# Adding the experts' rows to x: loads with adds on two engines, replaced by accumulating DMAs

## The chip, the cores and the metric

The kernel runs on one core of a Trainium2 chip. The metric is the device time of one execution in microseconds (us); lower is better. Everything is computed in float32.

## The reference, cut to what matters

Two blocks on 1024 tokens of 1024 numbers. The first block (a state-space layer, pooling, a gated unit and a dense FFN) and the first half of the second one (convolution and gated linear attention) are the same in both kernels. What the change touches is the end: a hierarchical mixture of experts, with a residual and a layer norm.

```
x = layer_norm(...)                         # 1024 tokens x 1024
gl = x @ w_group                            # softmax over 8 groups, one group a token
el = x @ w_expert, in the chosen group      # 8 experts, the best two (k = 0, 1)
for each token and its two experts e, weight w:
    h   = silu(x @ Wg[e]) * (x @ Wu[e])     # 1024 -> 512
    ffn += w * (h @ Wd[e])                  # 512 -> 1024
out = layer_norm(ALPHA * x + ffn) * g + b
```

There are 64 experts, each with 6.3 MB of weights (three matrices of 1024 x 512), so 403 MB in all.

## The kernel before, in words

**Sets.** The experts run in 30 sets, in the order of the string `ORDER` (line 33). A letter is a kind of set: F has the two experts that are fixed, D one expert with room for 256 tokens, S one expert with 128 tokens, P two experts with 64 tokens each, Q four experts with 32 tokens each. Which experts these are is found at run time, from the counts. The last five sets are P Q S S Q.

**Weights.** SP issues all weight loads, in the order of the sets, into a ring of eight chunks of 2 MB (`E.chunk`). A load into a chunk waits until the matmuls that read its former content are through. For a Q set the third matrix comes in 16 pieces of 512 KB by k (the call with `by_k`, line 1967). What stands behind a waiting load on SP waits as well.

**One set.** `fetch` gathers the next set's tokens from DRAM (`take`, an indirect DMA on POOL's queue) into one of two tiles `xg0`, `xg1`; `turn` transposes them on PE to `xT`. `hidden` does the gate and up products (`pg`, `pu`, line 1997), ACT the Silu (line 2004), DVE the product (line 2005). `rows` transposes h (`ph`, line 2013; copies to `hT`, lines 2016 and 2017), does the down-projection (`py`, line 2022) and scales the rows by the tokens' weights.

**Where the rows go.** For the first 27 sets ACT writes the scaled rows to a tile y, and `put` (line 1677) scatters y to the DRAM array `y2d`, in which token t has two rows, 2t for k = 0 and 2t + 1 for k = 1. The last `NLATE` = 3 sets don't scatter: their rows are added to x by products with a one-hot matrix S on PE (`spread`, its adds from PSUM on DVE at line 2052). For the last set of all only its own tokens' sums are wanted, in PSUM (`px`).

**Adding y2d to x.** Ahead of the weights of the penultimate set, `add(c)` runs for c = 0 to 3: SP loads 2 x 1 MB of y2d into a chunk of the ring (line 2102), and DVE and POOL add the two rows of each token to the eight tiles of x in SBUF (`xr`, 128 tokens each; line 2106).

**Norms and the end.** In the last set, `norms(range(4))` stands ahead of `hidden` and `norms(range(4, 8))` behind it. For each tile: two statistics and an aggregate on DVE (line 2119), a scaled copy by ACT into `xg0` or `xg1` (line 2126), a product by a row of gains (`io`) on DVE (line 2127), a sum with a row of offsets (`xT`) on POOL (line 2128), a store on POOL's queue (line 2129). So two tiles are in flight at a time. Last come the last set's tokens: their sums in `px` are normalised (line 2202) and scattered over the rows that the stores wrote (line 2206). Two loops behind this (`further` and the one at line 2213) serve experts with more tokens than their room; with the data here neither runs.

**Order on an engine.** A scheduler orders each engine's instructions by what it estimates of their times. It is not the order in which the code is written: instructions of `norms` can stand behind those of `hidden`.

Of the kernel before, what the change touches and what calls it, by code (L numbers as in the profile page):

```python
# [11 lines left out]
F32 = mybir.dt.float32  # L12
F32R = mybir.dt.float32r
BF = mybir.dt.bfloat16
I32 = mybir.dt.int32
# [3 lines left out]
P = 128  # L19
# [10 lines left out]
NLATE = 3  # L30
KINDS = {"F": (62, 64, 2), "D": (0, 2, 1), "S": (2, 12, 1), "P": (12, 30, 2), "Q": (30, 62, 4)}
CUT = (4,)
ORDER = "FQDPPQDPPQSSPQSQSPSQSPSPSPQSSQ"
# [1647 lines left out]
def route(tc, K, RT):  # L1681
# [225 lines left out]
    K.io, K.io128 = K.A4("io"), io128  # L1907
# [36 lines left out]
def experts(tc, I, K, out):  # L1944
# [64 lines left out]
    def rows(R, h, parts, w, between=lambda t, bank: None):  # L2009

        ph = PT("ph")
        for k in range(4):
            pe.transpose(ph[:, k * P:(k + 1) * P], h[:, k * P:(k + 1) * P], ident)
        hT = Z("hT", (P, 4, P), bufs=2)
        p4 = ph.rearrange("p (k t) -> p k t", k=4)
        dve.tensor_copy(hT[:, 0:2], p4[:, 0:2])
        dve.tensor_copy(hT[:, 2:4], p4[:, 2:4])
        py = [PT("py") for _ in range(2)]
        for k in range(4):
            for j in range(2):  # L2020
                for r, ws in parts:
                    pe.matmul(py[j][r], hT[:, k, r], ws[2][:, k, j], start=(k == 0), stop=(k == 3))  # L2022
                between(2 * k + j, PS)
        if len(R) == 1:
            for j in range(2):
                act.activation(R[0][:, hs[j]], py[j], AF.Copy, scale=w)  # L2026
            return
        for j in range(2):
            K.H.split_scaled(R[1][:, j], R[2][:, j], py[j], w)

    def places(again=True):
        if again:
            nc.sync.dma_start(K.io[:, 0:P], I["cmoe"][:, 8:8 + P])
        for t in range(again, 8):
            pool.tensor_scalar(K.io[:, t * P:(t + 1) * P], K.io[:, 0:P] if again else K.io128, float(t * P), None, op0=OP.add)

    def one_hot(S, tok):
        dve.tensor_scalar(S.rearrange("p a b -> p (a b)"), K.io, tok, None, op0=OP.is_equal)

    def spread(R, tok):  # L2040

        S, yh, yl = R
        if tok is not None:
            one_hot(S, tok)

        def part(t, bank=PS):
            o = S[:, t // 4, t % 4 * P:(t % 4 + 1) * P]
            for j in range(2):
                pa, x = bank("pa"), K.xa[t][:, hs[j]]
                pe.matmul(pa, o, yh[:, j], start=True, stop=False)  # L2050
                pe.matmul(pa, o, yl[:, j], start=False, stop=True)
                dve.tensor_tensor(x, x, pa, op=OP.add)

        return part
# [14 lines left out]
    def further(nb):  # L2069

        r = E.chunk(dt=F32R).rearrange("p (r a b) -> p r a b", a=2, b=512)
        r = [r[:, i] for i in range(3)]
        with tc.For_i(0, nb, 1) as it:
            e = nc.sync.value_load(K.bexp[0:1, bass.ds(it, 1)], min_val=0, max_val=63)
            ix, fx = Z("ix", (P, 1), I32, bufs=1), Z("fx", (P, 2), bufs=1)
            for o, a in ((ix, K.xdx), (fx[:, 0:1], K.tokf), (fx[:, 1:2], K.wtab)):
                nc.sync.dma_start(o, a[:, bass.ds(it + NCOL, 1)])
            ws, = weights([e])
            parts = [(full, ws)]
            rows(r, hidden([turn(fetch(ix))], parts)[0], parts, fx[:, 1:2])  # L2080
            places()
            add = spread(r, fx[:, 0:1])
            for t in range(8):
                add(t)

# [3 lines left out]
    none = nxt = lambda t, bank: None  # L2089
# [3 lines left out]
    n_late = len(order) - NLATE  # L2093
    ys, n_y = [K.A4("y0"), K.A4("y1")], 0
    S = K.A4("S", (P, 2, 512), F32R)

    def add(c):

        y = E.chunk().rearrange("p (t k d) -> p t k d", t=2, k=2)
        for j in range(2):  # L2100
            t = 2 * c + j
            nc.sync.dma_start(y[:, j], K.y2d[2 * t * P:2 * (t + 1) * P, :].rearrange("(p k) d -> p k d", k=2))
        for j in range(2):
            for k in range(2):
                x = K.xa[2 * c + j]
                (dve if j == 0 or k < c % 2 else pool).tensor_tensor(x, x, y[:, j, k], op=OP.add)
# [5 lines left out]
    def norms(ts):  # L2112

        n = len(ts)
        mv = Z("zmv", (P, n, 2), bufs=2)
        for i, t in enumerate(ts):
            st = Z("zst", (P, 2, 6), bufs=2)
            for j in range(2):
                dve.bn_stats(st[:, j], K.xa[t][:, hs[j]])
            dve.bn_aggr(mv[:, i], st)  # L2120
        rv, nm = Z("zrv", (P, n), bufs=2), Z("znm", (P, n), bufs=2)
        K.H.rstd_of(rv, mv[:, :, 1], 1, 1e-5, Z("zrt", (P, n), bufs=2))
        dve.scalar_tensor_tensor(nm, mv[:, :, 0], -1.0, rv, op0=OP.mult, op1=OP.mult)
        for i, t in enumerate(ts):
            o = xg[t % 2]
            act.activation(o, K.xa[t], AF.Identity, scale=rv[:, i:i + 1], bias=nm[:, i:i + 1])
            dve.tensor_tensor(o, o, row[0], op=OP.mult)
            pool.tensor_tensor(o, o, row[1], op=OP.add)
            nc.gpsimd.dma_start(out[t * P:(t + 1) * P, :], o)
# [3 lines left out]
    for i, rs in enumerate(order):  # L2133
        last = i == len(order) - 1
        if i == len(order) - 2:
            for c in range(4):
                add(c)
# [4 lines left out]
        if i == 0:  # L2142
            pool.memset(xg[1], 0.0)
            places(False)
            K.close_pool("q")
            E.grow()
        if i == n_late:
            R = [S] + [K.A4(n, (P, 2, 512), F32R) for n in ("yh", "yl")]
        if last:

            tok = col(K.tokf, cols(rs)[0])
            one_hot(R[0], tok)
            row = [K.io, xTs[turned[0] % 2].rearrange("p k t -> p (k t)")]
            row_load()
            same = Z("same", (P, P), F32R)
            norms(range(4))
        h = hidden(xT, parts, nxt)
        nxt = none
        xT = [turn(x) for x in xs]
        if last:  # L2160
            ST = []
            for j in range(2):
                pq = PT("pst")
                for t in range(4):
                    pe.transpose(pq[:, t * P:(t + 1) * P], S[:, j, t * P:(t + 1) * P].bitcast(F32), ident)
                ST.append(Z("hT", (P, 4, P), bufs=2))
                act.activation(ST[j], pq.rearrange("p (t s) -> p t s", t=4), AF.Copy)
            pq = PT("psame")
            for t in range(8):
                pe.matmul(pq[:, 0:P], ST[t // 4][:, t % 4], ST[t // 4][:, t % 4], start=(t == 0), stop=(t == 7))  # L2170
            dve.tensor_copy(same, pq[:, 0:P])
            px = [PS("px") for _ in range(2)]
            for t in range(8):
                for j in range(2):
                    pe.matmul(px[j], ST[t // 4][:, t % 4], K.xa[t][:, hs[j]], start=(t == 0), stop=False)
            norms(range(4, 8))
            act.activation(Z("zsq", (P, 1)), tok, AF.Sqrt)
        for j, c in enumerate(cols(rs)):
            if i < n_late:
                y = ys[n_y % 2]  # L2180
                n_y += 1
                rows([y], h[j], parts, col(K.wtab, c))
                put(nc, K, y, col(K.ydx, c))
            else:
                rows(R, h[j], parts, col(K.wtab, c), *[nxt] * (j > 0))
                if not last:
                    nxt = spread(R, col(K.tokf, c))
        if i == len(order) - 2:
            for t in range(8):
                nxt(t, (PS, PT)[t % 2])  # L2190
            nxt = none
# [3 lines left out]
    for j in range(2):  # L2195
        for y in R[1:]:
            pe.matmul(px[j], same, y[:, j], start=False, stop=(y is R[2]))
        dve.bn_stats(st[:, j], px[j])
    dve.bn_aggr(mv, st)
    x = xg[1]  # L2200
    for j in range(2):
        dve.scalar_tensor_tensor(x[:, hs[j]], px[j], mv[:, 0:1], row[0][:, hs[j]], op0=OP.subtract, op1=OP.mult)
    K.H.rstd_of(rv, mv[:, 1:2], 1, 1e-5, Z("lrt", (P, 1)))
    for j in range(2):
        dve.scalar_tensor_tensor(x[:, hs[j]], x[:, hs[j]], rv, row[1][:, hs[j]], op0=OP.mult, op1=OP.add)
    nc.gpsimd.indirect_dma_start(out=out, out_offset=bass.IndirectOffsetOnAxis(ap=col(K.xdx, cols(order[-1])[0]), axis=0), in_=x, in_offset=None,  # L2206
# [4 lines left out]
    nr = nc.values_load(K.nblk[0:1, 1:2], min_val=0, max_val=1)  # L2211
    further(nb)
    with tc.For_i(0, nr, 1):
        places()
        add = spread(R, tok)
        for t in range(8):
            add(t)
        row_load()
        for t in (0, 4):
            norms(range(t, t + 4))  # L2220
# [67 lines left out]
```

## Time and profile before

| | before |
|---|---|
| runs, us | 3242.50, 3233.73, 3240.19 (median 3240.19) |
| profiled execution, us | 3245.51 |
| its span, first to last instruction, us | 3243.8 |
| mean granted TensorE clock | 0.958 of full speed |
| PE, PEld busy | 2961.4 us (91%), 2091.7 us (64%) |
| DVE, ACT, POOL busy | 1631.6 us (50%), 845.2 us (26%), 771.7 us (24%) |
| HBM read, written | 584.19 MB, 85.98 MB |

The profile is taken from one execution, so sums over its rows compare with 3245.51, not with the median. PE, DVE, ACT and POOL are the compute engines, PEld is PE's weight load, SP issues DMAs. A tile in DRAM has a name that ends in _d or _dram. PE's 91% is a mean over stages that differ: before the experts PE works on the dense layers, and in the expert sets, from about 2200 us on, it runs beside a stream of weights. Matmuls are pipelined, and the time of a busy PE there says little on what it waits for.

### The profile page before, as it was taken

Reading aid. Unit: us, or ns where it says so; the run is one execution under the profiler, and the core shown is the slowest. Engines: PE = TensorE matmul, PEld = TensorE weight load, DVE = VectorE, ACT = ScalarE, POOL = GpSimd, SP = SyncE. Lnnn points to the kernel's source line nnn. Section 1 sums busy time; section 2 is a strip of 40 time slices with the busy share of each in tenths; the row PEclk is TensorE's granted clock in tenths of the full one; section 3 lists DMA queues with packets and bytes.
Section 4 is the critical chain, followed back from the end, with each engine's and each line's share of the span. In section 5 each row is a group of like instructions: output and inputs, shape, how many; then the busy total and the mean of one; then the engine's idle time right before and its main releaser. Section 6 shows DMA issues by size and latency. Waiting matters only on the chain. (4 is left out here: it accounts for less than half of the span.)

```text
span 3243.8 us, 39826 instructions
## 1 busy us (share of the span) xinstructions
PE 2961.4 (91%) x15247; PEld 2091.7 (64%) x15247; DVE 1631.6 (50%) x2686; ACT 845.2 (26%) x1447; POOL 771.7 (24%) x602
## 2 busy tenths in 40 slices
PE   8789989999999899999889999988989888989886
PEld 7779968888888678768778788963423322323232
DVE  7765495555567899885788554460000000000044
ACT  4233343333211533334332532121101010101002
POOL 4521174333200333334442142011000000000023
PEclk8899999999999899999899999989999999999998
DMA  3012222222622323323112574449999999999995
GB/s 123 17 49 96 79 78 78 86 89 93 240 92 91 117 91 106 109 72 105 65 61 72 173 247 168 168 187 420 390 422 396 422 414 415 426 396 426 386 399 231
DMA packets 135699, 656.61 MB, mean 202 GB/s; under 512 B 18826, under 2 KB 32010, under 8 KB 113873
## 3 DMA queue, kind: packets, MB, share of 16 engines
q1 hardware_dynamic: 118096, 610.50, 48.7%
q0 software_dynamic: 15104, 39.33, 3.1%
q10 hardware_dynamic: 2304, 4.20, 0.4%
q8 instruction: 121, 1.98, 0.3%
q14 instruction: 74, 0.60, 0.1%
HBM read 584.19 MB, written 85.98 MB: 207 GB/s over the span
## 5 line engine op out<-in xcount | busy, mean ns | idle before, releaser
L1997 PE MATMUL pg<-w,xT 128*32 128x512 f32 (+2 forms) x1056 | 349.3, 627 | 83.3 <-DMA w<-in_we_dram 83.3
L2005 DVE TENSOR_TENSOR h<-h,pu 128x512 f32<-128x512 f32 x32 | 22.0, 688 | 801.1 <-PE pu L1997 801.1
L1997 PE MATMUL pu<-w,xT 128*32 128x512 f32 (+2 forms) x1056 | 342.5, 618 | 0.0
L2022 PE MATMUL py<-w,hT 128*32 128x512 f32 (+2 forms) x1056 | 278.3, 604 | 19.4 <-issue 15.6
L1997 PEld LDWEIGHTS pg<-w,xT 128*32 128x32 f32 (+2 forms) x1056 | 96.8, 139 | 250.8 <-issue 127.3
L1997 PEld LDWEIGHTS pu<-w,xT 128*32 128x32 f32 (+2 forms) x1056 | 104.5, 140 | 168.1 <-issue 165.0
L2022 PEld LDWEIGHTS py<-w,hT 128*32 128x32 f32 (+2 forms) x1056 | 98.3, 136 | 167.5 <-issue 145.4
L320 POOL TENSOR_TENSOR ws<-wr 128x512 f32<-128x512 f32 x74 | 115.0, 1559 | 273.4 <-DMA wr<-in_w2T_dram 133.3
L1110 DVE TENSOR_TENSOR x<-x,pd 128x512 f32<-128x512 f32 x176 | 118.3, 686 | 75.0 <-PE pd L189 74.2
L179 DVE TENSOR_TENSOR ol<-ws,oh 128x512 fp32r<-128x512 f32 x148 | 128.3, 868 | 44.1 <-ACT oh L178 37.8
L2004 ACT ACTIVATE h<-pg 128x512 f32<-128x512 f32 x32 | 19.1, 597 | 458.0 <-PE pg L1997 416.9
L1677 POOL DMA_INDIRECT y_d<-y,ydx x29 | 29.0, 999 | 438.6 <-ACT y L2026 438.6
L178 ACT ACTIVATE oh<-ws 128x512 fp32r<-128x512 f32 x148 | 92.1, 625 | 140.6 <-PE pm L188 132.8
L1671 POOL DMA_INDIRECT xg<-x_d,xdx x31 | 31.7, 1023 | 396.9 <-PE pxg L1984 396.3
L188 PE MATMUL pd<-wdl,aoh 128*128 128x512 f32 x320 | 123.7, 391 | 0.0
L189 PE MATMUL pd<-wdh,aol 128*128 128x512 f32 x320 | 123.5, 390 | 0.0
L187 PE MATMUL pd<-wdh,aoh 128*128 128x512 f32 x320 | 121.0, 394 | 0.1
L179 DVE TENSOR_TENSOR ol<-wr,oh 128x512 fp32r<-128x512 f32 x117 | 109.1, 933 | 6.3 <-ACT oh L178 4.1
L178 ACT ACTIVATE oh<-wr 128x512 fp32r<-128x512 f32 x117 | 72.9, 626 | 119.8 <-PE pm L188 110.0
L179 POOL TENSOR_TENSOR wl<-wrB,wh 128x512 fp32r<-128x512 f32 x40 | 60.5, 1535 | 183.1 <-ACT wh L178 183.1
L1212 DVE SCALAR_TENSOR_TENSOR cadve<-cadve,vec 128x512 f32<-128x512 f32 x105 | 101.9, 971 | 0.1
L1212 DVE SCALAR_TENSOR_TENSOR cudve<-cudve,vec 128x512 f32<-128x512 f32 x105 | 98.2, 935 | 0.8
(831 smaller groups left out, 7965.2 us busy)
## 6 DMA issues: line engine op xcount, KB each, us to landing
w<-in_we_dram SPq DMA_DIRECT2D x160, 2048.0 KB, 23.8
w<-in_we_dram SPq DMA_DIRECT2D x128, 512.0 KB, 10.8
wr<-in_w2T_dram SPq DMA_DIRECT2D x34, 512.0 KB, 3.9
wr<-in_wg_dram SPq DMA_DIRECT2D x22, 512.0 KB, 3.3
wr<-in_wu_dram SPq DMA_DIRECT2D x22, 512.0 KB, 4.1
act_d<-go SPq DMA_DIRECT2D x22, 512.0 KB, 2.9
wrD<-act_d SPq DMA_DIRECT2D x22, 512.0 KB, 3.5
wrD<-in_wd_dram SPq DMA_DIRECT2D x22, 512.0 KB, 4.3
```

Source lines behind the costliest of these rows:

```text
L178: act.activation(hi, src, AF.Copy)
L179: (eng or dve).tensor_tensor(lo, src, hi.bitcast(F32), op=OP.subtract)
L187: pe.matmul(ps, l[0], r[0], start=(k == 0), stop=False)
L188: pe.matmul(ps, l[0], r[1], start=False, stop=False)
L189: pe.matmul(ps, l[1], r[0], start=False, stop=(k == n - 1))
L320: self.pool.tensor_tensor(s, self.s[a], self.s[b], op=op)
L1110: dve.tensor_tensor(xs, xs, pd, op=OP.add)
L1212: dve.scalar_tensor_tensor(o, x, w, c, op0=OP.mult, op1=OP.add)
L1671: nc.gpsimd.indirect_dma_start(out=x, out_offset=None, in_=K.x2d, in_offset=bass.IndirectOffsetOnAxis(ap=ix, axis=0), bounds_check=T - 1, ...
L1677: nc.gpsimd.indirect_dma_start(out=K.y2d, out_offset=bass.IndirectOffsetOnAxis(ap=ix, axis=0), in_=y, in_offset=None, bounds_check=2 * T - ...
L1997: pe.matmul(p[r], x[:, k, r], ws[k4][:, k % 4, j], start=(k == 0), stop=(k == 7))
L2022: pe.matmul(py[j][r], hT[:, k, r], ws[2][:, k, j], start=(k == 0), stop=(k == 3))
```

## The change

The order of the last five sets is P S S Q Q in place of P Q S S Q. All sets but the last scatter their rows to y2d, so there are no one-hot products any more. Behind the penultimate set's scatter POOL's queue has, in this order: one indirect accumulating load of the last tokens' first rows into their own tile `xl` (holding ALPHA * x), 16 accumulating DMAs that add 128 rows of y2d each to the tiles of x in SBUF (`gathered`: tiles 0 to 3 with k = 0, the same tiles with k = 1, then tiles 4 to 7), and the second indirect load. The norms run in place in x with two DVE instructions of one pass each, in pairs of tiles, and the stores read x. The last set's rows reach `xl` through one product with a matrix that says which rows belong to one token (`same`). One loop for overfull experts takes the place of two; it does not run here either.

```diff
-ORDER = "FQDPPQDPPQSSPQSQSPSQSPSPSPQSSQ"
+ORDER = "FQDPPQDPPQSSPQSQSPSQSPSPSPSSQQ"
...
-        if len(R) == 1:
-            for j in range(2):
-                act.activation(R[0][:, hs[j]], py[j], AF.Copy, scale=w)
-            return
         for j in range(2):
-            K.H.split_scaled(R[1][:, j], R[2][:, j], py[j], w)
+            act.activation(y[:, hs[j]], py[j], AF.Copy, scale=w)
...
-    def add(c):
-        y = E.chunk().rearrange("p (t k d) -> p t k d", t=2, k=2)
-        for j in range(2):
-            t = 2 * c + j
-            nc.sync.dma_start(y[:, j], K.y2d[2 * t * P:2 * (t + 1) * P, :].rearrange("(p k) d -> p k d", k=2))
-        for j in range(2):
+    def gathered():
+        for t4 in (0, 4):
             for k in range(2):
-                x = K.xa[2 * c + j]
-                (dve if j == 0 or k < c % 2 else pool).tensor_tensor(x, x, y[:, j, k], op=OP.add)
+                for t in range(t4, t4 + 4):
+                    src = K.y2d[2 * t * P:2 * (t + 1) * P, :].rearrange("(p k) d -> p k d", k=2)
+                    nc.gpsimd.dma_start(K.xa[t], src[:, k], accum_op=OP.add)
...
-        dve.scalar_tensor_tensor(nm, mv[:, :, 0], -1.0, rv, op0=OP.mult, op1=OP.mult)
         for i, t in enumerate(ts):
-            o = xg[t % 2]
-            act.activation(o, K.xa[t], AF.Identity, scale=rv[:, i:i + 1], bias=nm[:, i:i + 1])
-            dve.tensor_tensor(o, o, row[0], op=OP.mult)
-            pool.tensor_tensor(o, o, row[1], op=OP.add)
-            nc.gpsimd.dma_start(out[t * P:(t + 1) * P, :], o)
+            x = K.xa[t]
+            dve.scalar_tensor_tensor(x, x, mv[:, i, 0:1], row[0], op0=OP.subtract, op1=OP.mult)
+            dve.scalar_tensor_tensor(x, x, rv[:, i:i + 1], row[1], op0=OP.mult, op1=OP.add)
+            nc.gpsimd.dma_start(out[t * P:(t + 1) * P, :], x)
...
-        if i == len(order) - 2:
-            for c in range(4):
-                add(c)
...
-            one_hot(R[0], tok)
-            row = [K.io, xTs[turned[0] % 2].rearrange("p k t -> p (k t)")]
+            tok, xl = col(K.tokf, c), xg[(fetched[0] - 1) % 2]
+            row = [xg[fetched[0] % 2], xTs[turned[0] % 2].rearrange("p k t -> p (k t)")]
             row_load()
-            norms(range(4))
+            dve.tensor_scalar(xl, xl, ALPHA, None, op0=OP.mult)
+            gx = Z("gx", (P, 2), I32)
+            for k in range(2):
+                dve.tensor_scalar(gx[:, k:k + 1], tok, 2.0, float(k), op0=OP.mult, op1=OP.add)
+                nc.gpsimd.indirect_dma_start(out=xl, out_offset=None, in_=K.y2d, in_offset=bass.IndirectOffsetOnAxis(ap=gx[:, k:k + 1], axis=0),
+                                             bounds_check=2 * T - 1, oob_is_err=False, compute_op=OP.add)
+                if k == 0:
+                    gathered()
+            same = Z("same", (P, P))
+            dve.tensor_copy(same, tok.to_broadcast([P, P]))
+            for t in (0, 2):
+                norms((t, t + 1))
-        h = hidden(xT, parts, nxt)
+        h = hidden(xT, parts)
...
-            for t in range(8):
-                for j in range(2):
-                    pe.matmul(px[j], ST[t // 4][:, t % 4], K.xa[t][:, hs[j]], start=(t == 0), stop=False)
-            norms(range(4, 8))
+            dve.tensor_scalar(same, pq[:, 0:P], tok, None, op0=OP.is_equal)
+            norms((4, 5))
...
+    norms((6, 7))
...
-        for y in R[1:]:
-            pe.matmul(px[j], same, y[:, j], start=False, stop=(y is R[2]))
-        dve.bn_stats(st[:, j], px[j])
+        px = PS("px")
+        pe.matmul(px, same, y[:, hs[j]], start=True, stop=True)
+        dve.tensor_tensor(xl[:, hs[j]], xl[:, hs[j]], px, op=OP.add)
+        dve.bn_stats(st[:, j], xl[:, hs[j]])
```

The order on POOL of the kernel before, at the end of the experts: the last scatter of y, POOL's share of the adds of loaded rows to the tiles of x (xr), the two loads of the norms' rows (in_rows4), then sums and stores by turns.

```order
L1677 DMA y2_d_7385<-y0_19313,ydx_19202 2048x1024
L2106 TENSOR_TENSOR xr_17650<-xr_17650,w_22760 128x1024 x2
L2106 TENSOR_TENSOR xr_17654<-xr_17654,w_22767 128x1024
L2106 TENSOR_TENSOR xr_17658<-xr_17658,w_22774 128x1024 x2
L2106 TENSOR_TENSOR xr_17662<-xr_17662,w_22781 128x1024
L2110 DMA xT0_18957<-in_rows4_dram 128x1024
L2110 DMA io_19263<-in_rows4_dram 128x1024
L2128 TENSOR_TENSOR xg0_18956<-xg0_18956,xT0_18957 128x1024
L2129 DMA out_0_dram<-xg0_18956 128x1024
```

The order on POOL of the changed kernel at the same place, from the scatters of the sets S and Q on.

```order
L2056 DMA xg1_19272<-in_rows4_dram 128x1024
L1676 DMA y2_d_7385<-y1_19313,ydx_19202 2048x1024
L2056 DMA xT0_18957<-in_rows4_dram 128x1024
L1676 DMA y2_d_7385<-y0_19312,ydx_19202 2048x1024
L2097 DMA xg0_18956<-y2_d_7385,gx_22897 128x1024
L2052 DMA xr_17648<-y2_d_7385 128x1024
L2052 DMA xr_17650<-y2_d_7385 128x1024
L2052 DMA xr_17652<-y2_d_7385 128x1024
L2052 DMA xr_17654<-y2_d_7385 128x1024
L2052 DMA xr_17648<-y2_d_7385 128x1024
```

POOL's adds are gone; the accumulating DMAs stand behind the last scatter on its queue, and behind all 16 of them the second indirect load, the eight stores and the last scatter to the output.

The order on DVE of the kernel before, around the last set's hidden product (h, line 2005); xg0 and xg1 are the norms' two buffers, py the down-projection's PSUM.

```order
L2127 TENSOR_TENSOR xg0_18956<-xg0_18956,io_19263 128x1024
L2005 TENSOR_TENSOR h_23177<-h_23177,pu_23112 128x512
L2127 TENSOR_TENSOR xg1_19273<-xg1_19273,io_19263 128x1024
L2016 COPY hT_23274<-ph_23269 128x256
L2017 COPY hT_23274<-ph_23269 128x256
L2127 TENSOR_TENSOR xg0_18956<-xg0_18956,io_19263 128x1024
L2127 TENSOR_TENSOR xg1_19273<-xg1_19273,io_19263 128x1024
L183 SCALAR_TENSOR_TENSOR yl_22703<-py_23277,wtab_19246,yh_22702 128x512
```

The order on DVE of the changed kernel around that product (now line 2003); xr_17660 and xr_17662 are the last two tiles of x, xg1 and xT0 the rows of gains and offsets.

```order
L2066 BN_AGGR zmv_23117<-zst_23122 128x2
L192 TENSOR_SCALAR zrt_23127<-zmv_23117 128x2
L2071 SCALAR_TENSOR_TENSOR xr_17662<-xr_17662,zmv_23117,xg1_19272 128x1024
L195 RECIPROCAL zrv_23126<-rsq_23129 128x2
...
L199 TENSOR_TENSOR zrv_23126<-zrv_23126,rsq_23129 128x2
L2072 SCALAR_TENSOR_TENSOR xr_17660<-xr_17660,zrv_23126,xT0_18957 128x1024
L2072 SCALAR_TENSOR_TENSOR xr_17662<-xr_17662,zrv_23126,xT0_18957 128x1024
L2003 TENSOR_TENSOR h_23040<-h_23040,pu_22975 128x512
L2014 COPY hT_23078<-ph_23073 128x256
L2015 COPY hT_23078<-ph_23073 128x256
```

Before, three products of the norms stand behind h; now all norms of all eight tiles stand ahead of it.

## Rows read from the trace of the kernel before

**Rows 1.** The page's slices: 40 equal parts of the span.

```profile
DMA  3012222222622323323112574449999999999995
GB/s 123 17 49 96 79 78 78 86 89 93 240 92 91 117 91 106 109 72 105 65 61 72 173 247 168 168 187 420 390 422 396 422 414 415 426 396 426 386 399 231
```

**Rows 2.** Windows: us; busy us of PE, PEld, DVE, ACT, POOL; clock; DMA share; GB/s.

```profile
3185.00:3190.00 5.00, 5.00 (x13) 1.69 (x11) 1.19 (x2) 0.00 (x0) 4.55 (x3) 1.00 1.03 410
...
3200.00:3205.00 5.00, 3.70 (x24) 0.86 (x19) 1.22 (x1) 1.54 (x2) 1.40 (x2) 1.00 0.48 193
```

**Rows 3.** Timelines of the tail: start, duration, instruction [idle before <-releaser].

```profile
3207.25 0.60 ACT L2004 ACTIVATE h<-pg 128x512 f32<-128x512 f32 x1
3208.43 0.67 DVE L2005 TENSOR_TENSOR h<-h,pu 128x512 f32<-128x512 f32 x1
3209.16 1.11 PE L2013 MATMUL ph<-ident,h 128*128 128x128 f32 x4 [5.46 <-DVE h L2005]
...
3210.71 1.24 ACT L2126 ACTIVATE xg<-xr,znm,zrv 128x1024 f32<-128x1024 f32 x1 [2.86 <-DMA out_dram<-xg]
3211.98 1.23 DVE L2127 TENSOR_TENSOR xg<-xg,io 128x1024 f32<-128x1024 f32 x1 [2.88 <-ACT xg L2126]
3213.59 8.55 PE L2022 MATMUL py<-w,hT 128*32 128x512 f32 x64 [3.33 <-DVE hT L2016]
...
3230.12 1.41 DVE L2202 SCALAR_TENSOR_TENSOR xg<-px,lmv,io 128x512 f32<-128x512 f32 x2 [4.17 <-DMA out_dram<-xg]
...
3234.54 1.02 POOL L2206 DMA_INDIRECT out_dram<-xg,xdx  x1 [8.72 <-DVEq L2073]
```

**Rows 4.** The stream's hole: a window, SP's waits by line, timelines of POOL and SP.

```profile
3095.00:3100.00 5.00, 5.00 (x13) 2.20 (x12) 0.00 (x0) 0.00 (x0) 0.00 (x0) 1.00 0.14 58
...
SPq L2102 <- DMA y_d<-y,ydx: 19.3, 1, 19.3
...
3088.55 0.99 POOL L1677 DMA_INDIRECT y_d<-y,ydx  x1 [44.47 <-ACT y L2026]
...
3099.10 4.01 SPq L2102 DMA_DIRECT2D w<-y_d  x8
```

**Rows 5.** PE's timeline: first matmuls of the last sets (gate, up, transposes).

```profile
2990.07 1.13 PE L1997 MATMUL pg<-w,xT 128*128 128x512 f32 x2
...
3013.17 1.07 PE L1997 MATMUL pg<-w,xT 128*64 128x512 f32 x2
...
3015.03 1.09 PE L1984 MATMUL pxg<-ident,xg 128*128 128x128 f32 x8
...
3041.94 1.07 PE L1997 MATMUL pg<-w,xT 128*32 128x512 f32 x6
...
3050.55 1.09 PE L1997 MATMUL pu<-w,xT 128*32 128x512 f32 x3
```

**Rows 6.** DMA issues after 3040 us: count, KB each, median us to landing.

```profile
out_dram<-xg POOLq DMA_DIRECT2D x8, 512.0 KB, 3.7
xT<-in_rows_dram POOLq DMA_DIRECT2D x1, 512.0 KB, 10.6
y_d<-y,ydx POOLq DMA_INDIRECT x2, 10.9
```

**Rows 7.** The page's DMA queues: packets, MB, share of 16 engines' span.

```profile
q1 hardware_dynamic: 118096, 610.50, 48.7%
q0 software_dynamic: 15104, 39.33, 3.1%
```

**Rows 8.** DVE's groups by line after 2040 us: xcount | busy, mean ns | idle before.

```profile
L1657 DVE SCALAR_TENSOR_TENSOR xr<-xr,rv,row 128x1024 f32<-128x1024 f32 x8 | 10.3, 1285 | 0.3
L1656 DVE SCALAR_TENSOR_TENSOR xr<-xr,mv,row 128x1024 f32<-128x1024 f32 x8 | 10.2, 1275 | 0.0
...
L2119 DVE BATCH_NORM_STATS2 zst<-xr 128x6 f32<-128x512 f32 x16 | 10.1, 663 | 0.0
...
L199 DVE TENSOR_SCALAR rsq<-rsq 128x1 f32<-128x1 f32 x9 | 1.4, 154 | 0.3
```

## What I expected of it, before the changed kernel had run

> **What bounds the kernel now.** I read the page's slices first: from the middle of the span on, the DMA share stands at 9 tenths and the traffic near 390 to 426 GB/s up to the last slice, where it falls to 5 tenths [rows 1]. That stretch is the 30 expert sets, 64 experts of 6.3 MB each, and it is bound by the weight stream. A change there is worth something only if it shortens the stream, or the tail after it. So I then looked at the tail: the windows fall from 410 to 193 GB/s at 3200 us [rows 2] and the span ends at 3243.8. The tail of some 42 us is what remains when nothing streams. A page's "chain that ended last" is no help, since it breaks off at the last instruction; I followed the tail by each engine's timeline.
>
> In the tail [rows 3]: the activation of the last hidden product runs at 3207.3, the product at 3208.4, but the last down-projection starts only at 3213.6, because DVE stands in a norm that waits for ACT, ACT for an output store. Down-projection 8.6 us, then at 3230.1 a wait of 4.2 us for another store that frees xg1, the last scatter at 3234.5, and 9.3 us from there to the end. So about 10 us of the tail are waits that the norms' shared buffers cause. And the stream itself has one hole: in 3095 to 3100 it moves 58 GB/s, because the y loads on SP waited 19.3 us for the scatter issued at 3088.6, and everything behind them on SP with them [rows 4].
>
> **What is taken away.** The one-hot products, their 32 PSUM adds on DVE and the 16 adds of loaded y, on DVE and POOL, lie beside the weight stream; I cost their removal at nothing. Their cover is the stream itself. The y loads (8.4 MB, 20 us at 420 GB/s) leave SP, and so does the hole (about 5 us). But the bytes are not gone: the same 8.4 MB come on POOL's queue. The two late one-expert sets and the late four-expert set now scatter as well, at most 0.5 MB each; those are 1 to 4 us of stream, inside the estimates below.
>
> **The new order S S Q Q.** PE needs for a one-expert set 3013.2 - 2990.1 = 23.1 us, with the transposes of the next tokens 24.2 [rows 5]; the stream needs 15. Before, the two of them were fed beside 20 us of y loads. Now they follow the two-expert set directly, from 3041.9: PE is through at 3090.3. The ring has eight 2-MB chunks, so the eighth chunk of the next four-expert set waits for the second one's down-projection, and its 16 pieces of w2 wait for its own first pass, 9.7 us [rows 5], that is until 3100. Two us to start and 20 for 8.4 MB: this set is in at 3122. Had the stream not run dry, it would be in at 3110: before, 15 of these 18 chunks were in when the hole began at about 3095 [rows 4], and three more take 15 us. Loss: 12 us (bounds 0 and 15, the latter if the pieces also wait for a cold first pass). Its rows: last products 2 us after, two activations, scatter issued at about 3126, landing 10.9 later as before [rows 6], 3137. This is the wait on which the 16 accumulates hang, and POOL queues both indirect loads, all accumulates and all stores behind it.
>
> **The accumulates against the last weights.** At 3140, some 3 us after the first issue, 18 us of the last set's 25.2 MB have come (7.6 MB); 17.6 MB remain. On the software queue stand 16 x 0.52 MB and two indirect loads, about 8.9 MB. Both queues cost the same engine time per byte (48.7% of the span for 610.5 MB, 3.1% for 39.33 MB: 2.59 and 2.56 us per MB) [rows 7], and the engines are full, so time is conserved: all is in at 3140 + (17.6 + a x 8.9) / 0.42 us (0.42 MB per us), where a is the price of an accumulated byte in plain bytes. No row shows an accumulating DMA. The lower bound is a plain transfer, a = 1: 3203. It has to fetch the addend and the old x and to write x, so I take two plain passes, a = 2: 3224; three passes, a = 3: 3246. A single software load amid the stream took 10.6 us against 3.7 for a store outside it [rows 6], so the gather does not overtake the weights; it ends near them. Because the last 8.4 MB of weight pieces are issued only after the last set's first pass, they outlast it a little: I put the last tile 10 us ahead of the end (estimate; 5 for a = 1, 14 for a = 3, for the engine time that it then shares): 3198, **3214**, 3232.
>
> The Trainium skill, "Collectives: The Full Stack", section on the bandwidth ceiling, says that an add inside a DMA needs two source reads and gives 62.28 GB/s without and 32.35 with it, a ratio of 1.93. No run here shows it yet; with that ratio in place of my 2 the sum would come out 1.5 us earlier, with the plain price of the rows 16 us earlier.
>
> **The tail after the last tile.** The built order has every norm ahead of the last hidden product on DVE (front part, second pair of rows); so nothing of the last set goes on before x7 has landed. After it: two statistics at 0.66, six in-place products at 1.28 (two of them left over from the pair before), and ten short ones, 1.9 with the waits between them (estimate from 0.154 each), in all 10.9 us [rows 8]. Then the hidden product 0.7; transposes and copies 1.9 (from 3209.16 undisturbed, an estimate); down-projection 8.6; and from its end (3222.1) to the end of the span (3243.8) as before without the 4.2 us wait, 17.5 [rows 3]; plus two adds from PSUM, 1.4. One loop at the end instead of two: minus 1.5 (bounds 0 and 3, no row separates it). Sum 39.5, against 42 after the stream before: the waits on stores are gone, but 11 us of norms have come onto the path. 3214 + 39.5 = 3253.5.
>
> **Rivals.**
> 1. *The accumulates are as cheap as plain loads, and hidden: faster.* For it: equal price per byte on both queues [rows 7], and the last set's stream gives 60 us of cover. Against it: the 10.6 us [rows 6], and that an add has a second operand. Stream and gather end at 3203. It decides where the last tile lands 22 us or more ahead of the last weight piece (39.5 less 17.4 from the end of the down-projection): then the end is 3203 + 2 + 17.4 = 3222 by span, 3219 by the run. With the last tile at 3198 it is 3237, 3234 by the run. I give it 3226.
> 2. *Three passes or more: clearly slower.* 3232 + 39.5 = 3271.5, 3268 by the run. For it: POOL starts each second addition only after the first has landed; against it: four to eight are in flight.
> 3. *The stream does not run dry.* If PE's two one-expert sets are hidden by a lead of the stream, everything comes 12 us earlier: 3241.5, 3238 by the run, no change. For it: the stream was ahead of PE there (the four-expert set waited just 0.2 us for its weights). Against it: the ring holds only 40 us.
>
> **How the numbers follow.** The profiled execution took 3245.5, 1.7 over its span; the median of the runs is 3240.2, 5.3 below it. A span of 3253.5 is thus a run of 3249.9, say 3250: 0.3% over before, which is also about what a measurement of this kernel can tell from no change. Chances: the forecast 0.45 (its own range 3242 to 3258: 0.20 within 0.3%, 0.25 slower), rival 1 0.25 (0.18 faster, 0.07 within), rival 2 0.15 (slower), rival 3 0.15 (0.12 within, 0.02 faster, 0.01 slower). Faster 0.20, same 0.39, slower 0.41. The range goes from 3226, the middle of rival 1, to 3276, eight above rival 2; outside it lie the better half of rival 1 and the worst of rival 2, together under 0.2.
>
> **What the changed profile would show.** The stream's hole moves from 3095 to about 3087 to 3102, ahead of the penultimate set's last pieces. The first accumulate is issued near 3137, the last near 3210; its packets' time per MB is twice that of plain ones; the last DVE norms stand before the hidden product, which waits for them while PE idles some 30 us. I am wrong if the accumulates finish while weights still stream and DVE is idle at the hidden product (rival 1), if an accumulate takes much over 20 us to land (rival 2), or if the weight stream shows no gap before the last two sets (rival 3).

## The result and the profile after

| | before | changed |
|---|---|---|
| median of the runs, us | 3238.40 (4 runs) | 3261.09 (4 runs) |
| profiled execution, us; its span | 3245.51; 3243.8 | 3254.20; 3252.5 |

The ratio is 1.0062 with a 95% interval of 1.0049 to 1.0075, so the changed kernel is slower by 0.6%. Two further comparisons gave 1.0068 (1.0056 to 1.0081) and 1.0059 (1.0046 to 1.0071).

Spans don't compare well here, because the stage ahead of the experts, which the change leaves alone, takes some us more or less from one execution to the next. I therefore measure from a marker inside the expert stage: the start of the first 16 cut loads of a four-expert set on SP. In three profiles of before it stands at 2219.63, 2213.57 and 2218.11 us, and the end 1024.2, 1022.8 and 1022.4 behind it; in three of the changed kernel at 2214.27, 2215.98 and 2215.81, and the end **1038.2, 1038.4 and 1037.7** behind it. From there on the change costs 15 us, to within 1 us. The marker's line in the first profile of each kernel, before, then changed:

```profile
2219.63 19.01 SPq L1967 DMA_DIRECT2D w<-in_we_dram  x16
```

```profile
2214.27 17.48 SPq L1965 DMA_DIRECT2D w<-in_we_dram  x16
```

The page's slices and queues of the changed kernel (answers to [rows 1] and [rows 7]):

```profile
DMA  3012222222622323322122574459999999999896
GB/s 122 17 53 91 79 78 89 86 85 97 241 85 84 117 98 117 111 69 94 59 74 92 175 239 149 171 240 420 399 410 403 425 416 415 418 406 424 358 373 201
...
q1 hardware_dynamic: 116944, 602.12, 48.4%
q0 software_dynamic: 17984, 48.31, 4.4%
```

8.4 MB have left the weights' queue q1, and 9.0 MB have come to q0, whose share of the engines' time rose from 3.1 to 4.4%. Two slices near the end move less than before, for two different reasons. In the third from the end (358 GB/s against 386) the engines are less busy, 8 tenths against 9: the stream has a hole. In the last but one (373 against 399) they are as busy as before. Windows of 5 us of the changed kernel show where (columns as in [rows 2]):

```profile
3085.00:3090.00 5.00, 5.00 (x43) 1.65 (x41) 0.00 (x0) 0.00 (x0) 0.00 (x0) 1.00 0.45 147
...
3195.00:3200.00 5.00, 0.00 (x0) 0.00 (x0) 0.00 (x0) 0.00 (x0) 1.77 (x3) 0.50 1.06 275
...
3205.00:3210.00 5.00, 0.00 (x0) 0.00 (x0) 4.46 (x8) 0.00 (x0) 0.89 (x2) 0.50 1.05 286
3210.00:3215.00 5.00, 0.00 (x0) 0.00 (x0) 5.00 (x14) 0.20 (x1) 0.17 (x1) 0.50 1.04 402
...
3220.00:3225.00 5.00, 1.12 (x4) 0.72 (x4) 3.65 (x8) 0.71 (x2) 1.06 (x2) 0.50 0.61 244
```

The hole is at 3085 to 3090; from 3165 to 3210 full engines move some 275 GB/s in place of 420; from 3210 on they move 402 again. The timelines of the tail (answers to [rows 3]):

```profile
3118.73 1.00 POOL L1676 DMA_INDIRECT y_d<-y,ydx  x1 [21.01 <-issue]
3129.93 1.65 POOL L2097 DMA_INDIRECT xg<-y_d,gx  x1 [10.20 <-DMA y_d<-y,ydx]
3131.01 4.17 POOL L2052 DMA_DIRECT2D xr<-y_d  x4
...
3198.19 0.84 POOL L2052 DMA_DIRECT2D xr<-y_d  x1 [2.92 <-DMA xr<-y_d]
...
3170.46 1.02 PE L1995 MATMUL pu<-w,xT 128*32 128x512 f32 x2
...
3205.54 0.69 DVE L2065 BATCH_NORM_STATS2 zst<-xr 128x6 f32<-128x512 f32 x1 [2.35 <-DMA xr<-y_d]
...
3213.97 0.63 DVE L2065 BATCH_NORM_STATS2 zst<-xr 128x6 f32<-128x512 f32 x1
...
3223.06 0.68 DVE L2003 TENSOR_TENSOR h<-h,pu 128x512 f32<-128x512 f32 x1
...
3223.79 1.12 PE L2011 MATMUL ph<-ident,h 128*128 128x128 f32 x4 [52.31 <-DVE h L2003]
3225.43 8.18 PE L2020 MATMUL py<-w,hT 128*32 128x512 f32 x64 [0.52 <-DVE hT L2014]
...
3242.79 1.03 POOL L2132 DMA_INDIRECT out_dram<-xg,xdx  x1 [18.82 <-DVEq L2137]
```

The last up-projection is through at 3171, and PE then waits 52.3 us for the hidden product, which stands behind all norms on DVE, and these wait for the gather. How long the accumulating loads take from their issue to their landing (least, median and most of the 16; then the median of the three issued between 3190 and 3200):

```profile
DMA to landing us min/median/max: 14.7/18.5/34.7
```

```profile
xr<-y_d POOLq DMA_DIRECT2D x3, 512.0 KB, 14.9
```

The last of them, issued at 3198.19, thus lands at about 3213.1, 999 us behind the marker. DVE has been busy all but without a break since 3205.5, when the second tile of the last four was in.

**The account from the marker to the end.** The share of each queue in that stretch, before, then changed:

```profile
q1 hardware_dynamic: 40736, 383.44, 90.0%
q0 software_dynamic: 9670, 20.31, 5.1%
```

```profile
q1 hardware_dynamic: 39549, 374.57, 87.0%
q0 software_dynamic: 12556, 29.29, 9.3%
```

Before, 95.1% of 1024.2 us is 974 us of work for the DMA engines on these two queues, and 50 us in which they have next to nothing to do, holes and tail together. Changed, 96.3% of 1038.2 is 1000 us of work and 38 us without. So the change adds 26 us of engine time and takes 12 us of empty time away. The bytes of the two queues hardly differ (403.8 MB before, 403.9 changed), so the 26 us are not more data.

### The profile page after: what moved, and what is told of

It is laid out like the page before. It is cut to its first block, busy times and chain, and to the rows that moved or that the text cites. A ratio compares the mean times of both kernels' runs of the same rounds, so it can differ in the third digit from the quotient of the medians.

```text
span 3252.5 us, 39425 instructions
## 1 busy us (share of the span) xinstructions
PE 2925.4 (90%) x15128; PEld 2064.6 (63%) x15128; DVE 1595.1 (49%) x2657; ACT 834.5 (26%) x1439; POOL 752.4 (23%) x600
## 5 line engine op out<-in xcount | busy, mean ns | idle before, releaser
L1670 POOL DMA_INDIRECT xg<-x_d,xdx x31 | 31.5, 1017 | 404.2 <-PE pxg L1982 403.0
L2023 ACT ACTIVATE y<-py,wtab 128x512 f32<-128x512 f32 x64 | 43.8, 687 | 252.9 <-PE py L2020 190.1
```

The source lines that it names most:

```text
L1670: nc.gpsimd.indirect_dma_start(out=x, out_offset=None, in_=K.x2d, in_offset=bass.IndirectOffsetOnAxis(ap=ix, axis=0), bounds_check=T - 1, ...
L2023: act.activation(y[:, hs[j]], py[j], AF.Copy, scale=w)
```

## The experiments

**The addition taken out of the gather.** The same 16 loads, which overwrite x.

```diff
-                    nc.gpsimd.dma_start(K.xa[t], src[:, k], accum_op=OP.add)
+                    nc.gpsimd.dma_start(K.xa[t], src[:, k])
```

> The changed kernel, its 16 gather DMAs without the addition: the same loads from DRAM on the same queue, which overwrite x in place of adding to it (the sums are left out of the output). Theory (an accumulated byte costs two plain ones of DMA engine time, so 8.4 MB of it cost some 20 us of a full stream): the last tile and the last weights come 16 to 20 us earlier, the time falls by 14 to 20 us, to about 3244. Rival (what counts is the bytes and the software queue, not the addition): no change, 3258 to 3264.

Median 3244.88 us, 14 less than the changed kernel's 3258.96 on the same chip; from the marker to the end 1022.5 in place of 1038.4, as in the kernel before. The two queues' share of that stretch is 95.5%, 976 us, so nearly all of the 26 us of engine time are gone. Its median is still 7 us over before's on that chip (ratio 1.0019, 1.0010 to 1.0029), which the distances from the marker don't show. The queues over 10 us in which gather and weights run side by side, changed (3190 to 3200), then without the addition (3175 to 3185):

```profile
q0 software_dynamic: 379, 1.37, 68.5%
q1 hardware_dynamic: 378, 1.38, 36.8%
```

```profile
q1 hardware_dynamic: 562, 2.04, 51.4%
q0 software_dynamic: 562, 2.04, 51.3%
```

The gather costs 10 x 0.685 / 1.37 = 5.0 us of the 16 engines for a MB with the addition and 10 x 0.513 / 2.04 = 2.5 without: a ratio of 2.0. The Trainium skill ("Collectives: The Full Stack", the section on the bandwidth ceiling) gives 1.93 between a collective that copies and one whose DMAs add; this trace agrees to within 4%. The theory holds: the addition, not the bytes or the queue, is what costs, 14 to 16 us.

**The norms behind the hidden product.** `norms` for all tiles is called in `rows` of the last set, behind the copies to `hT` on DVE, and the last rows' scaling stands behind the last root on ACT. The main lines of the edit:

```diff
+        if last:
+            with tc.issue_after(turned_h.ins):
+                for t in (0, 2, 4, 6):
+                    norms((t, t + 1))
```

> The changed kernel with all norms behind the last hidden product and its two copies on DVE, and the last scaled rows behind the last root on ACT. Theory (the hidden product waits 52 us for norms that wait for the gather; the last weight pieces land at about 3217): the last down-projection ends near 3219 in place of 3233.6, and the time falls by 9 to 13 us, to about 3250. Rival (the last norms and stores are the end by themselves, with the sum for the last tokens behind them on DVE): falls by 0 to 4 us.

Median 3250.35, 8.6 less than the changed kernel on that chip, just under the 9 to 13 of the theory, and 12.2 less from the marker to the end (1026.2); still behind the kernel before, by a ratio of 1.0040 (1.0025 to 1.0054). Timelines of PE and DVE:

```profile
3177.44 0.66 PE L2011 MATMUL ph<-ident,h 128*128 128x128 f32 x4 [0.85 <-DVE h L2003]
...
3226.04 1.90 PE L2020 MATMUL py<-w,hT 128*32 128x512 f32 x4 [0.58 <-SPq L2136]
...
3226.90 2.48 DVE L2076 SCALAR_TENSOR_TENSOR xr<-xr,zrv,xT 128x1024 f32<-128x1024 f32 x2
3229.30 1.33 DVE L2125 TENSOR_TENSOR xg<-xg,px 128x512 f32<-128x512 f32 x2
```

The down-projection now follows the weight pieces, in steps, from 3178.6 on, and ends at 3227.9, some 1.5 us ahead of the last norms; both are late because of the transfers. So the norms' place on DVE is worth 9 to 12 us; the addition, with 14 to 16, costs more than that. No run takes both away, so the two can't simply be added up.

**The old order of sets in the changed kernel.**

```diff
-ORDER = "FQDPPQDPPQSSPQSQSPSQSPSPSPSSQQ"
+ORDER = "FQDPPQDPPQSSPQSQSPSQSPSPSPQSSQ"
```

> The changed kernel with the order of sets of before (P Q S S Q in place of P S S Q Q at the end). Theory (the two one-expert sets straight behind the two-expert set let the weight stream run dry, 10 us in the windows from 3060 to 3095): the windows ahead of the last two sets stay near 420 GB/s, the gather starts later against the weights but the engines stay full, and the time falls by 8 to 12 us against the changed kernel, to about 3251. Rival (the chain of accumulating DMAs is long by itself, 81 us from its first issue to its last landing, whatever runs beside it): it starts at about 3136 and ends at about 3217, the time is 3262 to 3268, not faster.

Median 3262.82 beside 3258.96, and 1041.7 from the marker to the end in place of 1038.4: nothing gained, rather 3 us lost. My theory was wrong in its result, though the stream did become denser: in 3020 to 3100 the engines are busy for 0.97 of the time, against 0.91. But the gather begins 933.5 us behind the marker in place of 916.7, and now the weights are in before the last tile is. The rival's time came (3262 to 3268), but not its reason: the loads take some 68 us from the first issue to the last landing, not 81. A window and the queues in it:

```profile
3200.00:3210.00 10.00, 0.00 (x0) 0.00 (x0) 0.00 (x0) 0.00 (x0) 4.00 (x6) 0.50 1.05 202
```

```profile
q0 software_dynamic: 516, 1.86, 100.3%
q1 hardware_dynamic: 46, 0.16, 4.4%
```

What the order saves in the hole it gives back, since x, not the weights, is what the norms wait for. With the norms moved behind the hidden product I tried it again:

> The changed kernel with the norms behind the hidden product and with the order of sets of before. With the norms ahead the old order gained nothing: its last weights came 8 us earlier from the marker, its last tile of x 3 us later. Theory (the last tile and the norms behind it are the end, not the weights): here too nothing is gained against 3250.4, 3250 to 3255. Rival (with the norms out of the way the end is the last weight piece and the down-projection): 7 to 9 us less, about 3242.

Median 3251.14, 1028.8 from the marker, against 3250.35 and 1026.2 with the new order: again nothing, as the last tile and its norms are the end.

**The new order alone, in the kernel before.** The same line of `ORDER`, the other way round.

> The kernel before with the new order of sets alone (P S S Q Q at the end). Theory (the order by itself costs: SP's loads of y2d now wait for the scatter of a one-expert set that PE works off more slowly than the stream comes): the hole in the stream grows from 5 to 10 or 15 us, the time rises by 5 to 12 us, to about 3246. Rival (the order is free, as undoing it in the changed kernel gained nothing): 3235 to 3241.

Median 3255.68 against 3242.41 for before on that chip, ratio 1.0040 (1.0027 to 1.0053): 13 us slower, a little more than expected, and 11 us more from the marker to the end (1034.1). SP's wait, and two windows:

```profile
SPq L2102 <- DMA y_d<-y,ydx: 39.0, 1, 39.0
```

```profile
3040.00:3050.00 10.00, 10.00 (x25) 4.50 (x24) 0.00 (x0) 0.00 (x0) 0.27 (x1) 1.00 0.19 77
3050.00:3060.00 10.00, 8.59 (x23) 3.72 (x23) 1.45 (x3) 0.60 (x1) 0.00 (x0) 1.00 0.01 2
```

The y loads wait 39.0 us in place of 19.3 [rows 4], with the weights behind them. The order that costs 11 to 13 us there costs nothing in the changed kernel. The wait stands there on POOL's queue, with no weights behind it; that this is the reason fits the waits and was not tested by itself.

**The norms in place, alone, in the kernel before.** Two products on DVE for a tile and stores from x, behind the matmuls that read x.

> The kernel before with one part of the change alone: its norms in place, two products on DVE for a tile, all behind the matmuls that read x, stores from x. Theory (some 10 us of the tail of before are waits for stores that free the two buffers, and this part of the change takes them away): the last down-projection starts near 3209 in place of 3213.6, the wait of 4.2 us behind it is gone, the time falls by 7 to 11 us, to about 3229. Rival (DVE's in-place products, 20 us of them, stand ahead of the hidden product and take the gain back): 3236 to 3242.

Median **3229.95**, ratio 0.9956 (0.9940 to 0.9971) to before: faster than both kernels, by 12.5 us against before on that chip; from the marker to the end it is 1014.2, 9 less than the mean of before. The tail (compare [rows 3]):

```profile
3205.84 0.66 PE L2013 MATMUL ph<-ident,h 128*128 128x128 f32 x4 [0.85 <-DVE h L2005]
3208.56 7.12 PE L2022 MATMUL py<-w,hT 128*32 128x512 f32 x64 [2.07 <-DVE hT L2016]
...
3223.94 1.02 POOL L2204 DMA_INDIRECT out_dram<-xg,xdx  x1 [14.93 <-DVEq L2073]
```

The waits for stores are gone, and the last scatter comes at 3223.9 in place of 3234.5, with the marker 0.3 us earlier. This is the part of the change that gains. The edit also calls the norms of the first four tiles later than before, so what their place and what the missing waits are worth is not told apart.

**The y loads moved to POOL's queue, on top of that.**

```diff
-            nc.sync.dma_start(y[:, j], K.y2d[2 * t * P:2 * (t + 1) * P, :].rearrange("(p k) d -> p k d", k=2))
+            nc.gpsimd.dma_start(y[:, j], K.y2d[2 * t * P:2 * (t + 1) * P, :].rearrange("(p k) d -> p k d", k=2))
...
-                (dve if j == 0 or k < c % 2 else pool).tensor_tensor(x, x, y[:, j, k], op=OP.add)
+                dve.tensor_tensor(x, x, y[:, j, k], op=OP.add)
```

> The same, with the eight loads of y2d issued on POOL's queue in place of SP's, and all 16 additions on DVE. Theory (the stream's hole at 3095, 4.7 us, is SP waiting for the last scatter with weights queued behind): the hole closes, 3 to 6 us less than the norms in place alone, about 3225. Rival (the loads that wait are late, and the ring's chunks that they hold are then missing to the weights): the same or slower, 3229 to 3238.

Median 3244.64, 14.7 slower than without it, and slower than the theory (3225) and the rival (3229 to 3238) had it; from the marker to the end 1025.5, 11 more. The hole at 3095 closes (387 GB/s in 3090 to 3100), and a larger one opens. A window, and waits of DVE, PE and SP in 3085 to 3150:

```profile
3130.00:3140.00 10.00, 10.00 (x24) 4.47 (x23) 7.38 (x8) 1.37 (x2) 0.00 (x0) 0.92 0.20 57
```

```profile
DVE xr L2106 <- DMA w<-y_d: 43.5, 3, 37.3
```

```profile
PE ph L2013 <- DVE h L2005: 24.4, 1, 24.4
```

```profile
SPq L1937 <- PE py L2022: 31.9, 1, 31.9
```

The loads share the engines with weights and land late; DVE stands 37.3 us in an addition with a hidden product queued behind it, PE waits for that, and SP for PE's chunks. The wait has moved from SP to DVE. As the edit also gives POOL's additions to DVE, the 11 to 15 us are those of both together.

**Both kernels again**, for further profiles and tighter ratios.

> The changed kernel once more, for a second profile and a tighter ratio. Its first profiled execution had a span of 3252.5 us, its other runs 3259 to 3260, and before the other way round (profiled 3243.8, others 3232 to 3241). Theory A: the 7 us lie in the dense stage ahead of the experts (before 2200 us), which the change doesn't touch, so a second profile has its last tile, stream end and tail at the same distances from the start of the expert stage as the first. Theory B: they lie in the last 120 us, where weights and accumulating DMAs share the engines, so a profile of a slower execution has its last tile later than 3211. Ratio to before 1.005 to 1.008.

> The kernel before once more, for a second profile. Measured from the first of the 16 cut weight loads of the first four-expert set (2219.63 us in its first profile) the end stood 1024.2 us later, in the two profiles of the changed kernel 1038.2 and 1038.4: 14 us between them, while the medians of the runs are 22 us apart. Theory A (the dense stage of the one profiled execution of before was slow by chance, some 8 us): this profile has its marker near 2212 to 2216 and its end again 1024 behind it. Theory B (executions of before differ in the expert stage, and the profiled one was a slow one there): the end stands 1014 to 1018 us behind the marker.

> The changed kernel a third time, beside the kernel before on the same chip. In two profiles of each the part from the marker (first of the 16 cut loads of the first four-expert set) to the end is 1038.3 against 1023.5 us, 15 us more; the medians of the runs are 20 to 23 us apart. Theory A: 15 us is the effect, and the rest is the spread of the stage ahead of the marker (2213.6 to 2221.9 us in ten profiles): the medians of this comparison are 14 to 18 us apart. Theory B: executions without a profile lose 20 to 23 us here too.

Medians: changed 3258.96 and 3258.40, before 3239.85. A third profile of before (median 3239.55; from marker to end 1022 to 1025 was expected, 1022.4 came) gave the third marker above. All markers of the runs in this document but one (2221.9, without the addition) lie in 2213 to 2220, and for one kernel the end is at nearly the same distance behind them. So the profiles show 15 us in the expert stage, while the medians of these two comparisons are 21 and 18 us apart. The marker did come early in the second profile of before and the distances held, as theory A of the first two runs said; but the 14 to 18 us between the medians, of theory A of the third, was just missed (18.2), and where the other 3 to 6 us lie no profile shows. Each of the three profiled executions of the changed kernel was the fastest among the executions timed with it, so what its slower executions lose, and in which stage, no profile shows.

## Why the prediction was right, and where it was not

The measured time lies in the range, and the sign is that of the forecast; but 3250 was 10 us over before, at the edge of what can be told from no change, and it became 18 to 23. Step by step, as distances from the marker of each profile (2219.63 for the predicted times, which were made on the first profile of before, 2214.27 for the changed kernel's):

- **The start of the gather** was forecast at 3137, 917 behind the marker; it is at 3131.0, 917.
- **The dry stream** was forecast at 3087 to 3102, 867 to 882 behind the marker; the hole is at 3085 to 3090, 871 to 876, and shorter than forecast, with thin stretches ahead of it. Rival 3, that it would not run dry, is out. But before runs dry as much: over 3020 to 3100 the engines are idle for 0.10 of the time before and 0.09 changed, 8 and 7 us. I had set 12 us of loss for the new order against one hole of 5; over these 80 us the two cancel.
- **The price of an accumulated byte**, taken as 2 between bounds of 1 and 3, measured 2.0. The last tile was forecast 994 behind the marker; it landed at 3213.1, 999, 4 us late. Rival 1's case, the same bytes at the plain price, was run: its span of 3237 is 1017 behind the marker, and the run without the addition ends 1022.5 behind its own, so this sum too was some 5 us short. Rival 2's sign, a load that takes much over 20 us to land, did show (34.7 at most), though the price is two: the first four loads are issued within 4.2 us and wait for one another, with weights beside them.
- **The tail.** From the last tile to the hidden product I had 10.9 us; it is 10.0. But the last tile alone does not set this: DVE is busy for 17.5 us on end ahead of the product, as it still works off the tiles before the last, and it reaches the last tile at 3213.2, just when that is in. The transposes, copies and the down-projection take 10.6 in place of 11.2, and from the down-projection's end to the span's end it is 18.9 in place of 17.4. The last tile's 4.5 us, less 0.9 and 0.7 and with 1.5 more, make up the 4 us by which 1038.2 is over the forecast 1033.9. PE's idle time ahead of the hidden product was put at some 30 us and is 52.3.
- **What was put at nothing.** The one-hot products and the adds that the change removes were costed at nothing. No run takes them out alone, so this stays unproven. Of scatters there are two more (31 in place of 29), for the two one-expert sets. The prediction counted a third, but the late four-expert set scattered before too.
- **From the profile to the median.** The forecast comes to 9.7 us more than before (3253.5 - 3243.8), added to the median. In the profiles the difference is 15.0 (means of three, 1038.1 and 1023.1): 4 us of what lacked are the last tile and the tail, 1 us is that the first profile of before was a little long. The medians differ by another 3 to 8 us, and that stays open. That the span itself came out at 3252.5, 1 us from the forecast, is chance: in that execution the marker came 5 us earlier than in the one I had worked from.

Rival 2, three passes and 3268, came nearer to the median than the forecast by luck; its mechanism was wrong: the price is two. The sign, too, was a near thing: the prediction gave 0.41 to slower and 0.39 to no change.

## What to carry to other kernels

A DMA that adds is no free adder where the transfers are the bound: it saves DVE and POOL time that lay idle and pays for it with the engines' time that was full. Look what a moved wait has queued behind it: the same order of sets cost nothing where the wait stood on POOL's queue and 11 to 13 us where it stood on SP's, ahead of weights; the y loads, moved the other way and with POOL's additions moved to DVE, cost 11 to 15 us, with a hidden product waiting behind them on DVE. Of a change with several parts each is worth a run alone: here the norms in place gain 0.4% by themselves, while the whole change loses 0.6%.

## What was not expected of the hardware

The two queues, with pieces of 4 KB, shared the engines packet for packet here: 379 packets of the gather and 378 of weights in 10 us, and 562 each without the addition. As the accumulating packet took twice as long, the gather held two thirds of the engines' time (68.5 against 36.8%), and the weights fell to 138 GB/s (1.38 MB in 10 us). Nearly alone (46 packets of weights beside 516), the accumulating loads filled all 16 engines and moved 186 GB/s (1.86 MB in 10 us at 100.3%).
